# The head of a fused transformer kernel: products of zeros on PE, a held load, and norm weights behind the transposes

## The chip, the cores and the metric

The kernel runs on one core of a Trainium2 chip. The metric is the device time of one execution in microseconds (us), the median of several runs. The engines are PE (TensorE, matrix products), DVE (VectorE), ACT (ScalarE), POOL (GpSimd) and SP (SyncE, which here issues the loads). SBUF is the memory on the core with 128 partitions; PSUM is the memory that PE writes its results to.

## The reference

The input `x` has 256 tokens of width 1024. A first block computes a SwiGLU feed-forward, a mixer (a gated linear recurrence and a windowed attention side by side) and a second feed-forward, each with a norm ahead of it and one behind it; a second block of two hybrid layers follows. The change touches only the beginning, which is

```python
def rms_norm(x, g):
    xf = x.astype(jnp.float32)
    y = xf * lax.rsqrt(jnp.mean(xf * xf, axis=-1, keepdims=True) + NORM_EPS)
    return (y * g.astype(jnp.float32)).astype(x.dtype)

def swiglu(x, w_gu, w_down):
    g, u = jnp.split(x @ w_gu, 2, axis=-1)
    return (jax.nn.silu(g) * u) @ w_down
...
    f = swiglu(rms_norm(h, ffn1_pre_g[l]), ffn1_w_gu[l], ffn1_w_down[l])
    h = h + MACARON_SCALE * rms_norm(f, ffn1_post_g[l])
```

with `w_gu` of 1024 x 5632 and `w_down` of 2816 x 1024, all in float32.

## The kernel before

The work runs in five phases: feed-forward, mixer, feed-forward, and two hybrid layers. The 256 tokens are two token tiles, t = 0 and 1, of 128 tokens each, whose residual stays in SBUF as `h0` and `h1`. Each phase normalizes a tile (`pre_norm`), transposes it on PE (`to_xT`), and then streams the weights from HBM in units of 512 KB.

Every product of two matrices is made of three (`mm3`, lines 224 to 226). An operand a is split into a rounded part ah (type fp32r, which PE multiplies in one pass) and the rest al = a - ah; the sum ah bh + ah bl + al bh takes the place of a b. For the weights this split is in `split_raw`: ACT casts the raw unit to its high part (line 207), DVE subtracts to get the low part (line 208). For the activations it is in `split` (lines 214 and 215). In the trace `raw` is a loaded unit, `w` its two parts, `xh` and `xl` the two parts of the transposed activations, `tp` the transposes in PSUM. There are 4 raw buffers and 8 w buffers, so unit 4 is loaded when the first raw buffer is free again.

The order on each engine is made by a scheduler. It takes the instructions by their place in the program, but lets a later one go ahead on an engine as long as the earlier one isn't ready by the scheduler's own account of time. Each engine then runs its instructions strictly in that order, and so does SP with its loads. `tc.issue_after(ins)` puts what a block traces on the engine of `ins` behind `ins` in that order; it adds no wait.

At the head of the program, `setup` loads tile 0 of x in two halves of 512 columns and the norm weights `ffn1_pre_g` as a broadcast, the same 4 KB row to all 128 partitions (`g`, 512 KB), and makes the identity for the transposes. `pre_norm(0)` squares on ACT (line 401), takes an inverse root on DVE in eight small operations (`root`), and multiplies h by the root and g on DVE (line 380, `hn`). `to_xT(0)` makes eight transposes on PE (line 391), four to a PSUM bank, and splits each bank into xh and xl.

The first feed-forward begins in `firstA` with two chunks of 512 columns, `ga` (gate) and `ua` (up), each with four units of 256 rows of `w_gu`. A unit is six products of 512 columns for each token tile. With `LEAD = 2` the program multiplies units 0 and 1 with token tile 0 first, then transposes tile 1, multiplies units 0 and 1 with tile 1, and takes the later units with both tiles in turn. Behind the chunks come pairs of 256 columns (`gu`), whose results stay transposed, and the down products (`dn`). When a chunk of ga is complete for a tile, ACT applies Silu to it (line 509). `run` walks through the generator of a phase with `next(cur)`: the first call loads the first units, the second multiplies the lead for tile 0, the third the rest.

The functions that the diff touches, with their callers:

Of the kernel before, what the change touches and what calls it, by code (L numbers as in the profile page):

```python
# [10 lines left out]
F32 = mybir.dt.float32  # L11
F32R = mybir.dt.float32r
I32 = mybir.dt.int32
AF = mybir.ActivationFunctionType
ALU = mybir.AluOpType
PSUM = bass.MemoryType.PSUM
P = 128
S = 256
D = 1024
# [3 lines left out]
SC = (1024 / 27) ** 2  # L23
EPS = 1e-6
# [7 lines left out]
AHEAD = 6  # L32
M_ORDER = 'xaxAxlxpPqLQ'
W_Q, W_C, W_D0, W_D = (10., 12., 14., 10.)
L_ORDER = 'v0mmma1b'
LEAD = 2
B_AFTER = 3
W_LRU, W_ML = (6.0,6.0)

# [3 lines left out]
NX = 3  # L43
W_SD = 8.0
W_X = 2.5


def host_constants():
# [48 lines left out]
class Kern:  # L97
    def __init__(self, tc, a, ex):
# [11 lines left out]
        self.now, self.live, self.last = 0.0, 0, None  # L110
        self.taken = deque([-W_X] * NX)
        self.lanes = {n: deque() for n in ("tp", "T", "S")}
# [37 lines left out]
    def room(self, n=1):  # L150

        while self.taken[n - 1] + W_X > self.now:
            yield 0.0, 0.3
# [85 lines left out]
    def root(self, v):  # L239

        nc = self.nc
        m = v.shape[1]
        s, t, p = (self.small([P, m], x) for x in ("rs", "rt", "rp"))
        stt, tt = nc.vector.scalar_tensor_tensor, nc.vector.tensor_tensor
        nc.vector.tensor_scalar(s.bitcast(I32), v.bitcast(I32), -0.5, float(0x5F3759DF - 2 ** 31), op0=ALU.mult, op1=ALU.add)

        def vss():
            if m == 1:  # L250
                stt(t, in0=s, scalar=v, in1=s, op0=ALU.mult, op1=ALU.mult)
            else:
                tt(t, s, s, op=ALU.mult)
                tt(t, t, v, op=ALU.mult)

        vss()
        stt(p, in0=t, scalar=-10.0 / 3, in1=t, op0=ALU.add, op1=ALU.mult)
        stt(s, in0=p, scalar=5.0, in1=s, op0=ALU.add, op1=ALU.mult)
        vss()
        stt(s, in0=t, scalar=-64.0 / 3, in1=s, op0=ALU.add, op1=ALU.mult)  # L260
        return s


    def setup(self):
        nc, a = self.nc, self.a
        c = self.const
        self.h = [c.tile([P, D], F32, name=f"h{t}") for t in range(2)]
        self.load_x(0)
        self.g_first = self.bcast(a["ffn1_pre_g"][0], "g0")
        self.id = c.tile([P, P], F32, name="ident")  # L270
        make_identity(nc, self.id)
        self.slots = {}

    def load_x(self, t):
        for f in range(2):
            c = slice(f * 512, (f + 1) * 512)
            self.nc.sync.dma_start(out=self.h[t][:, c], in_=self.a["x"][0, t * P:(t + 1) * P, c])

    def params(self):
        nc, a = self.nc, self.a  # L280
# [83 lines left out]
        xl = self.xp.tile([P, 8, S], F32R, tag="xl", name="xl")  # L364
        return xh, xl

    def pre_norm(self, t, g, late=False):

        nc = self.nc
        h = self.h[t]  # L370
        hn = self.b4([P, D], "hn")
        parts = [slice(q * 512, (q + 1) * 512) for q in range(2)]
        v = self.mean_square([h[:, c] for c in parts])
        if not late:
            for c in parts:
                nc.vector.tensor_tensor(hn[:, c], h[:, c], g[:, c], op=ALU.mult)
        rs = self.root(v)
        for c in parts:
            if late:
                ins = nc.vector.scalar_tensor_tensor(hn[:, c], in0=h[:, c], scalar=rs, in1=g[:, c], op0=ALU.mult, op1=ALU.mult)  # L380
            else:
                ins = nc.vector.tensor_scalar(hn[:, c], hn[:, c], rs, None, op0=ALU.mult)
            self.normed = ins.ins
        return hn

    def to_xT(self, t, hn, xT):
        sl = slice(t * P, (t + 1) * P)
        for q in range(2):
            ps = self.bank("x", "tp", (P, 4, P))
            for i in range(4):  # L390
                self.nc.tensor.transpose(ps[:, i], hn[:, (4 * q + i) * P:(4 * q + i + 1) * P], self.id)
            ins = self.split(xT[0][:, 4 * q:4 * q + 4, sl], xT[1][:, 4 * q:4 * q + 4, sl], ps)
        return ins

    def mean_square(self, parts):

        nc = self.nc
        ss = self.small([P, 2], "ss2")
        for i, x in enumerate(parts):
            junk = self.t([P, 512], "junk")  # L400
            nc.scalar.activation(junk, x, AF.Square, accum_out=ss[:, i:i + 1])
        v0, v = self.small([P, 1], "v0"), self.small([P, 1], "v")
        nc.vector.tensor_scalar(v0, ss[:, 0:1], SC / D, SC * EPS, op0=ALU.mult, op1=ALU.add)
        nc.vector.scalar_tensor_tensor(v, in0=ss[:, 1:2], scalar=SC / D, in1=v0, op0=ALU.mult, op1=ALU.add)
        return v

# [31 lines left out]
    def firstA(self, xT, chunks, evacs, lead=None):  # L438

        us = [(i, u) for i in range(len(chunks)) for u in range(4)]
        n0 = len(us) if lead is None else lead
        ws, accs = {}, {}
        for at, (i, u) in enumerate(us[:n0 if lead is None else 1]):

            with self.tc.issue_after(self.normed) if at >= AHEAD else nullcontext():
                ws[i, u] = chunks[i][0](u)
        yield

        def step(i, u, t):
            if (i, u) not in ws:
                ws[i, u] = chunks[i][0](u)
            if u == 0:
                accs[i, t] = self.bank("acc", chunks[i][2], (P, chunks[i][1]))
            self.stepA(accs[i, t], xT, ws[i, u], u, t)
            if u == 3:
                evacs(i, t, accs[i, t])

        for i, u in us[:n0]:  # L460
            step(i, u, 0)
        yield
        for i, u in us[:n0]:
            step(i, u, 1)
        for i, u in us[n0:]:
            for t in range(2):
                step(i, u, t)
# [671 lines left out]

    def run(self, out, stop=99):  # L1140
        nc, a = self.nc, self.a
        self.setup()
        ffn = lambda n, **kw: (FFN_POOLS, lambda x: self.ffn(x, a[f"ffn{n}_w_gu"][0], a[f"ffn{n}_w_down"][0], **kw))
        layer = lambda l: (LAYER_POOLS, lambda x: self.layer(l, x))
        phases = [(ffn(1, lead=LEAD, early=self.params), "ffn1_post_g", 0.5, a["mix_pre_g"][0]), ((MIXER_POOLS, self.mixer), "mix_post_g", 1.0, a["ffn2_pre_g"][0]),
                  (ffn(2), "ffn2_post_g", 0.5, a["norm_g_2"][0]), (layer(0), None, 0, a["norm_g_2"][1]), (layer(1), None, 0, None)]
        xT = self.new_xT()
        hn = [self.pre_norm(0, self.g_first, True)]
        chain = lambda t, acc: self.pre_norm(t, self.g_first, True)
        acc = None  # L1150
        cur = None
        for i, ((pools, start), post, scale, pre) in enumerate(phases):

            ph = self.phase(pools)
            ph.__enter__()
            cur = start(xT)
            next(cur)
            ins = self.to_xT(0, hn[0], xT)
            if i == 0:
                self.load_x(1)  # L1160
            with self.tc.issue_after(ins) if i == 0 else nullcontext():
                hn.append(chain(1, acc))
            next(cur)
            self.to_xT(1, hn[1], xT)
            acc = next(cur)
            if i == stop - 1 or i == len(phases) - 1:
                if post is None:
                    self.residual(0, acc, out)
                    self.residual(1, next(cur), out)
                else:  # L1170
                    gp = self.bcast(a[post][0], "gpost")
                    self.post_norm(0, acc, gp, scale)
                    self.post_norm(1, next(cur), gp, scale)
                    for t in range(2):
                        nc.sync.dma_start(out=out[t * P:(t + 1) * P], in_=self.h[t])
                ph.__exit__(None, None, None)
                return
            gp = self.bcast(a[post][0], "gpost") if post else None
            gn = self.bcast(pre, "gpre")

            def chain(t, acc, gp=gp, gn=gn, scale=scale):
                if gp is None:
                    self.residual(t, acc)
                else:
                    self.post_norm(t, acc, gp, scale)
                return self.pre_norm(t, gn)

            xT = self.new_xT()
            hn = [chain(0, acc)]
            acc = next(cur)  # L1190
            ph.__exit__(None, None, None)
# [138 lines left out]
```

## Time and profile before

| what | us |
|---|---|
| median of 3 runs | 1348.41 |
| lowest, highest | 1348.16, 1349.8 |
| the profiled execution | 1345.55 |
| its span, from the first to the last instruction | 1343.8 |

The profiled execution is one execution of its own beside the three runs; its span leaves out 1.75 us of its time. In the views below an instruction is named by engine, line of the program, operation and operands (written first, read behind the arrow), a shape and a count; a bracket tells how long its engine idled ahead of it, and what ended that. PEld is the load of the stationary operand on PE, which overlaps the products. A q behind an engine is its queue.

### The profile page before, as it was taken

What the parts mean: (1) busy time and instruction counts of PE and PEld (TensorE: products, weight loads), DVE (VectorE), ACT (ScalarE), POOL (GpSimd) and SP (SyncE); (2) the same over time, 40 slices, a digit from 0 to 9 for tenths busy, and PEclk for the clock granted to TensorE, in tenths of its full rate; (3) what the DMA queues carried; (4) which work ended last, traced back from release to release, by engine and by line L of the source; (5) the groups of instructions that cost most, each with busy time, mean ns of one, the idle gap of its engine ahead of it and who ended that gap; (6) DMA issues with size and microseconds to landing.
All of it is one profiled execution on the core that took longest, in us unless ns stands there. A gap on an engine that the chain in (4) does not pass through costs nothing.

```text
span 1343.8 us, 24690 instructions
## 1 busy us (share of the span) xinstructions
PE 1313.7 (98%) x9434; PEld 1215.6 (90%) x9434; DVE 948.5 (71%) x2178; ACT 784.5 (58%) x1468; POOL 3.0 (0%) x10
## 2 busy tenths in 40 slices
PE   6999999999999999999999999999999999999998
PEld 5899988989997899998998889999899988899997
DVE  6547667897868655568888676666788886765663
ACT  6444544788745544455667776554456667755451
POOL 0000000000000000000000000000000000000000
PEclk9999999999999999999999999999999999999999
DMA  7757764445565566673755454666656543546661
GB/s 255 226 166 234 224 219 142 139 146 135 169 213 179 176 197 191 205 231 98 212 142 131 126 173 126 180 186 194 179 157 186 142 128 104 173 145 187 193 195 52
DMA packets 234806, 230.30 MB, mean 171 GB/s; under 512 B 12336, under 2 KB 213184, under 8 KB 234688
## 3 DMA queue, kind: packets, MB, share of 16 engines
q1 hardware_dynamic: 232432, 227.05, 56.8%
q10 hardware_dynamic: 2256, 1.67, 0.5%
q8 instruction: 74, 1.21, 0.4%
q14 instruction: 44, 0.36, 0.1%
HBM read 227.64 MB, written 1.05 MB: 170 GB/s over the span
## 4 chain that ended last, share of the span: by engine, by line
PE 75%; DVE 11%; ACT 6%; DMA 5%; issue 2%; SPq 0%; ACTq 0%; DVEq 0%
PE gu L224 5%; PE gu L226 5%; PE gu L225 5%; PE gp L224 3%; DVE w L208 3%; PE gp L225 3%; PE gp L226 3%; PE dqk L224 3%; PE dqk L226 3%; PE dn L226 3%; PE dn L225 3%; PE dqk L225 3%; PE dn L224 3%; DMA raw<-in_w_in_dram 3%; PE po L224 2%
## 5 line engine op out<-in xcount | busy, mean ns | idle before, releaser
L208 DVE TENSOR_TENSOR w<-raw,w 128x1024 fp32r<-128x1024 f32 (+1 forms) x437 | 501.8, 1156 | 222.3 <-ACT w L207 218.5
L207 ACT CAST w<-raw 128x1024 fp32r<-128x1024 f32 (+1 forms) x437 | 433.3, 999 | 334.4 <-PE gu L226 51.1
L224 PE MATMUL gu<-xh,w 128*128 128x256 f32 x576 | 159.6, 277 | 0.0
L226 PE MATMUL gu<-xh,w 128*128 128x256 f32 x576 | 159.2, 276 | 0.0
L225 PE MATMUL gu<-xl,w 128*128 128x256 f32 x576 | 159.1, 276 | 0.0
L224 PE MATMUL dqk<-w,xh 128*128 128x384 f32 x384 | 136.5, 355 | 0.0
L225 PE MATMUL dqk<-w,xh 128*128 128x384 f32 x384 | 129.5, 337 | 0.0
L226 PE MATMUL dqk<-w,xl 128*128 128x384 f32 x384 | 129.2, 336 | 0.0
L225 PEld LDWEIGHTS gu<-xl,w 128*128 128x128 f32 x576 | 108.2, 188 | 0.6
L224 PEld LDWEIGHTS gu<-xh,w 128*128 128x128 f32 x576 | 108.1, 188 | 0.6
L224 PE MATMUL gp<-xh,w 128*128 128x256 f32 x384 | 108.3, 282 | 0.0
L226 PEld LDWEIGHTS gu<-xh,w 128*128 128x128 f32 x576 | 108.2, 188 | 0.0
L226 PE MATMUL gp<-xh,w 128*128 128x256 f32 x384 | 106.4, 277 | 0.0
L225 PE MATMUL gp<-xl,w 128*128 128x256 f32 x384 | 106.2, 277 | 0.0
L224 PEld LDWEIGHTS dqk<-w,xh 128*128 128x128 f32 x384 | 72.2, 188 | 6.2 <-issue 6.0
L224 PEld LDWEIGHTS gp<-xh,w 128*128 128x128 f32 x384 | 72.1, 188 | 2.7 <-issue 2.7
L225 PEld LDWEIGHTS dqk<-w,xh 128*128 128x128 f32 x384 | 72.4, 189 | 0.2
L226 PEld LDWEIGHTS gp<-xh,w 128*128 128x128 f32 x384 | 72.2, 188 | 0.0
L226 PEld LDWEIGHTS dqk<-w,xl 128*128 128x128 f32 x384 | 72.2, 188 | 0.0
L225 PEld LDWEIGHTS gp<-xl,w 128*128 128x128 f32 x384 | 72.2, 188 | 0.0
L226 PE MATMUL dn<-w,aT 128*128 128x512 f32 x176 | 69.1, 393 | 0.0
L225 PE MATMUL dn<-w,aT 128*128 128x512 f32 x176 | 68.9, 391 | 0.0
(378 smaller groups left out, 3242.6 us busy)
## 6 DMA issues: line engine op xcount, KB each, us to landing
raw<-in_w_in_dram SPq DMA_DIRECT2D x140, 512.0 KB
raw<-in_ffn_w_gu_dram SPq DMA_DIRECT2D x88, 512.0 KB
raw<-in_w_in_dram SPq DMA_DIRECT2D x192, 192.0 KB
raw<-in_ffn_w_down_dram SPq DMA_DIRECT2D x44, 512.0 KB
raw<-in_w_o_dram SPq DMA_DIRECT2D x16, 512.0 KB
raw<-in_w_proj_attn_dram SPq DMA_DIRECT2D x16, 256.0 KB
raw<-in_w_proj_lru_dram SPq DMA_DIRECT2D x8, 512.0 KB
raw<-in_w_out_dram SPq DMA_DIRECT2D x8, 512.0 KB
```

Of the source, the lines that this page charges most:

```text
L207: nc.scalar.copy(hi, raw)
L208: nc.vector.tensor_tensor(lo, raw, hi, op=ALU.subtract)
L224: m(out, lhsT=ah, rhs=bh, start=first, stop=False)
L225: m(out, lhsT=ah, rhs=bl, start=False, stop=False)
L226: self.last = m(out, lhsT=al, rhs=bh, start=False, stop=last).ins
```

## The change

- In `setup` the norm weights come as an 8 x 128 tile. PE transposes it to 128 x 8, and ACT copies it to `gT`, in which each partition has the weights of its eight columns of the transposed activations.
- `pre_norm` in the first phase only multiplies by the root, on ACT. The weights are applied in `to_xT`: DVE multiplies each bank of four transposes by `gT` into an SBUF tile `xg`, from which xh and xl are made.
- A tile of zeros is made on DVE. `spin(n)` multiplies it n times with itself on PE (128 x 128 by 128 x 256, float32); nobody reads the results. `SPIN` gives the counts: 2 at the start, 4 behind the transpose of the norm weights, 1 behind the transposes of tile 0, and 2, 1, 2, 2 behind the four units of the lead.
- `LEAD` is 4: all of ga is multiplied with tile 0 ahead of the transposes of tile 1. Unit 0 is loaded at the first `next(cur)`, units 1 and 2 at the second, in SP's order behind the load of tile 1 of x.
- The load of tile 1 of x comes behind two memsets of one column each of `h1`, which DVE runs behind the first small operation of tile 0's root.

```diff
-LEAD = 2
+LEAD = 4
+SPIN = (2, 4, 1, 2, 1, 2, 2)
...
 in root():
-        stt(s, in0=t, scalar=-64.0 / 3, in1=s, op0=ALU.add, op1=ALU.mult)
+        self.rooted = stt(s, in0=t, scalar=-64.0 / 3, in1=s, op0=ALU.add, op1=ALU.mult).ins
...
 in setup():
-        self.g_first = self.bcast(a["ffn1_pre_g"][0], "g0")
+        g = self.t([8, P], "g8")
+        nc.sync.dma_start(out=g, in_=a["ffn1_pre_g"][0].rearrange("(k p) -> k p", p=P))
         self.id = c.tile([P, P], F32, name="ident")
         make_identity(nc, self.id)
+        self.zero = self.tl("n", [P, 256], "zero")
+        nc.vector.memset(self.zero, 0.0)
+        self.spin(SPIN[0])
+        gp = self.bank("x", "gT", (P, 8))
+        self.last = nc.tensor.transpose(gp, g, self.id[0:8, 0:8]).ins
+        self.spin(SPIN[1])
+        return gp
+
+    def spin(self, n):
+        ps = self.bank("yp", "spin", (P, 256))
+        for _ in range(n):
+            with self.tc.issue_after(self.last) if self.last is not None else nullcontext():
+                self.nc.tensor.matmul(ps, lhsT=self.zero[:, 0:P], rhs=self.zero, start=True, stop=True)
...
 in pre_norm():
-            if late:
-                ins = nc.vector.scalar_tensor_tensor(hn[:, c], in0=h[:, c], scalar=rs, in1=g[:, c], op0=ALU.mult, op1=ALU.mult)
+            if g is None:
+                nc.scalar.activation(hn[:, c], h[:, c], AF.Copy, scale=rs)
...
 in to_xT():
+            src = ps
+            if gT is not None:
+                self.last = tr.ins
+                src = self.t([P, 4, P], "xg")
+                self.nc.vector.tensor_tensor(src, ps, gT[:, ks].unsqueeze(2).to_broadcast([P, 4, P]), op=ALU.mult)
+            ins = self.split(xT[0][:, ks, sl], xT[1][:, ks, sl], src)
...
 in firstA():
-        for at, (i, u) in enumerate(us[:n0 if lead is None else 1]):
+        for at, (i, u) in enumerate(us[:n0 if lead is None else 3]):
-            with self.tc.issue_after(self.normed) if at >= AHEAD else nullcontext():
+            with self.tc.issue_after(self.normed) if at >= AHEAD or lead is not None and at == 0 else nullcontext():
                 ws[i, u] = chunks[i][0](u)
+            if lead is not None and at == 0:
+                yield
         yield
...
-        for i, u in us[:n0]:
+        for at, (i, u) in enumerate(us[:n0]):
             step(i, u, 0)
+            if lead is not None:
+                self.spin(SPIN[3 + at])
...
 in run():
-        self.setup()
+        gp = self.setup()
...
-        hn = [self.pre_norm(0, self.g_first, True)]
-        chain = lambda t, acc: self.pre_norm(t, self.g_first, True)
+        gT = self.const.tile([P, 8], F32, name="gT")
+        nc.scalar.copy(gT, gp)
+        hn = [self.pre_norm(0, None)]
+        self.normed = self.rooted
+        chain = lambda t, acc: self.pre_norm(t, None)
+        with self.tc.issue_after(self.squared):
+            for f in range(2):
+                nc.vector.memset(self.h[1][:, f * 512:f * 512 + 1], 0.0)
...
             next(cur)
-            ins = self.to_xT(0, hn[0], xT)
             if i == 0:
                 self.load_x(1)
+            ins = self.to_xT(0, hn[0], xT, gT)
+            if i == 0:
+                self.spin(SPIN[2])
+                with self.tc.issue_after(ins), self.tc.issue_after(self.loaded):
+                    next(cur)
             with self.tc.issue_after(ins) if i == 0 else nullcontext():
                 hn.append(chain(1, acc))
-            next(cur)
-            self.to_xT(1, hn[1], xT)
+            with self.tc.issue_after(ins) if i == 0 else nullcontext():
+                next(cur)
+            self.to_xT(1, hn[1], xT, gT)
+            gT = None
```

`self.squared` is the first small operation of `mean_square` on DVE, `self.loaded` the load of the second half of tile 1.

## Rows read from the trace of the kernel before

**Rows 1.** The page's busy line: busy us, share of the span, instructions.

```profile
PE 1313.7 (98%) x9434; PEld 1215.6 (90%) x9434; DVE 948.5 (71%) x2178; ACT 784.5 (58%) x1468; POOL 3.0 (0%) x10
```

**Rows 2.** Timeline, PE, 9 to 20 us: start, us, engine, line, what.

```profile
9.65 1.94 PE L391 MATMUL tp<-ident,hn 128*128 128x128 f32 x8 [9.65 <-DVE hn L380]
...
11.56 0.80 PE L224 MATMUL ga<-w,xh 128*128 128x512 f32 x1
...
13.53 0.63 PE L224 MATMUL ga<-w,xh 128*128 128x512 f32 x1
...
13.96 0.63 PE L225 MATMUL ga<-w,xh 128*128 128x512 f32 x1
...
16.09 0.50 PE L225 MATMUL ga<-w,xh 128*128 128x512 f32 x1 [0.65 <-DVE w L208]
...
16.43 0.40 PE L226 MATMUL ga<-w,xl 128*128 128x512 f32 x1
...
18.27 1.07 PE L391 MATMUL tp<-ident,hn 128*128 128x128 f32 x8
...
19.55 0.51 PE L224 MATMUL ga<-w,xh 128*128 128x512 f32 x1
```

**Rows 3.** The same timeline, SP's issues, ACT and DVE, 0 to 13 us.

```profile
0.74 0.86 SPq L277 DMA_DIRECT2D h<-in_x_dram  x2
...
1.65 0.42 SPq L182 DMA_DIRECT2D g<-in_ffn_pre_g_dram  x1
2.12 0.43 SPq L188 DMA_DIRECT2D raw<-in_ffn_w_gu_dram  x1
2.59 1.04 SPq L277 DMA_DIRECT2D h<-in_x_dram  x2
3.46 0.63 ACT L401 ACTIVATE junk<-h 128x512 f32<-128x512 f32 x1 [1.45 <-DMA h<-in_x_dram]
...
4.11 0.63 ACT L401 ACTIVATE junk<-h 128x512 f32<-128x512 f32 x1
...
4.87 0.16 DVE L404 SCALAR_TENSOR_TENSOR v<-ss,v 128x1 f32<-128x1 f32 x1 [0.49 <-ACT junk L401]
...
6.14 0.16 DVE L260 SCALAR_TENSOR_TENSOR rs<-rt,rs 128x1 f32<-128x1 f32 x1
8.76 1.41 DVE L380 SCALAR_TENSOR_TENSOR hn<-h,rs,g 128x512 f32<-128x512 f32 x2 [2.46 <-DMA g<-in_ffn_pre_g_dram]
...
9.98 1.05 ACT L207 CAST w<-raw 128x1024 fp32r<-128x1024 f32 x1 [5.15 <-DMA raw<-in_ffn_w_gu_dram]
10.93 1.29 ACT L214 CAST xh<-tp 128x512 fp32r<-128x512 f32 x2
11.06 1.23 DVE L208 TENSOR_TENSOR w<-raw,w 128x1024 fp32r<-128x1024 f32 x1 [0.89 <-ACT w L207]
...
12.20 1.28 DVE L215 TENSOR_TENSOR xl<-tp,xh 128x512 fp32r<-128x512 f32 x2
```

**Rows 4.** Busy time by stretch, instructions of ga alone (count, clock, DMA share).

```profile
11.50:18.30 6.80, 6.09 (x16) 3.63 (x16) 0.00 (x0) 1.00 0.66 209
```

**Rows 5.** Groups by line on PE, 11.5 to 37.8 us.

```profile
L224 PE MATMUL ga<-w,xh 128*128 128x512 f32 x16 | 7.3, 454 | 0.0
...
L226 PE MATMUL ua<-w,xl 128*128 128x512 f32 x16 | 6.3, 394 | 0.0
```

**Rows 6.** Timeline, PE, 37 to 38 us.

```profile
37.76 0.28 PE L224 MATMUL gu<-xh,w 128*128 128x256 f32 x1
```

**Rows 7.** Timeline, PE, around 258 us.

```profile
257.74 0.59 PE L838 MATMUL lg<-xc,wab 128*128 128x256 f32 x2
258.17 0.59 PE L839 MATMUL lg<-xc,wab 128*128 128x256 f32 x2
```

**Rows 8.** The first timeline again, ACT, 25 to 27 us.

```profile
25.52 1.28 ACT L509 ACT_TABLE_LOAD   x1
...
26.82 0.60 ACT L509 ACTIVATE sa<-ga 128x512 f32<-128x512 f32 x1
```

More of the change, by code (lines that the diff above doesn't have):

```diff
@@ L268, in setup @@
         self.load_x(0)
-        self.g_first = self.bcast(a["ffn1_pre_g"][0], "g0")
+        g = self.t([8, P], "g8")
+        nc.sync.dma_start(out=g, in_=a["ffn1_pre_g"][0].rearrange("(k p) -> k p", p=P))
         self.id = c.tile([P, P], F32, name="ident")
         make_identity(nc, self.id)
-        self.slots = {}
+        self.zero = self.tl("n", [P, 256], "zero")
[10 more added lines that the diff above has]
+                self.nc.tensor.matmul(ps, lhsT=self.zero[:, 0:P], rhs=self.zero, start=True, stop=True)
     def load_x(self, t):
@@ L276, in load_x @@
             c = slice(f * 512, (f + 1) * 512)
-            self.nc.sync.dma_start(out=self.h[t][:, c], in_=self.a["x"][0, t * P:(t + 1) * P, c])
+            self.loaded = self.nc.sync.dma_start(out=self.h[t][:, c], in_=self.a["x"][0, t * P:(t + 1) * P, c]).ins
     def params(self):
@@ L365, in new_xT, with pre_norm @@
         return xh, xl
-    def pre_norm(self, t, g, late=False):
+    def pre_norm(self, t, g):
         nc = self.nc
@@ L373, in pre_norm @@
         v = self.mean_square([h[:, c] for c in parts])
-        if not late:
+        if g is not None:
             for c in parts:
@@ L378, in pre_norm, with to_xT @@
         for c in parts:
-            if late:
-                ins = nc.vector.scalar_tensor_tensor(hn[:, c], in0=h[:, c], scalar=rs, in1=g[:, c], op0=ALU.mult, op1=ALU.mult)
-            else:
-                ins = nc.vector.tensor_scalar(hn[:, c], hn[:, c], rs, None, op0=ALU.mult)
-            self.normed = ins.ins
+            if g is None:
+                nc.scalar.activation(hn[:, c], h[:, c], AF.Copy, scale=rs)
+            else:
+                self.normed = nc.vector.tensor_scalar(hn[:, c], hn[:, c], rs, None, op0=ALU.mult).ins
         return hn
-    def to_xT(self, t, hn, xT):
+    def to_xT(self, t, hn, xT, gT=None):
         sl = slice(t * P, (t + 1) * P)
         for q in range(2):
+            ks = slice(4 * q, 4 * q + 4)
             ps = self.bank("x", "tp", (P, 4, P))
             for i in range(4):
-                self.nc.tensor.transpose(ps[:, i], hn[:, (4 * q + i) * P:(4 * q + i + 1) * P], self.id)
-            ins = self.split(xT[0][:, 4 * q:4 * q + 4, sl], xT[1][:, 4 * q:4 * q + 4, sl], ps)
+                tr = self.nc.tensor.transpose(ps[:, i], hn[:, (4 * q + i) * P:(4 * q + i + 1) * P], self.id)
+            src = ps
[4 more added lines that the diff above has]
+            ins = self.split(xT[0][:, ks, sl], xT[1][:, ks, sl], src)
         return ins
@@ L402, in mean_square @@
         v0, v = self.small([P, 1], "v0"), self.small([P, 1], "v")
-        nc.vector.tensor_scalar(v0, ss[:, 0:1], SC / D, SC * EPS, op0=ALU.mult, op1=ALU.add)
+        self.squared = nc.vector.tensor_scalar(v0, ss[:, 0:1], SC / D, SC * EPS, op0=ALU.mult, op1=ALU.add).ins
         nc.vector.scalar_tensor_tensor(v, in0=ss[:, 1:2], scalar=SC / D, in1=v0, op0=ALU.mult, op1=ALU.add)
```

## The prediction

> **What bounds the kernel now.** I read the page's busy shares first, then the timeline of the first 45 us engine by engine, then the count and the spacing of the first phase's products, and last single rows for prices. The page says that PE is busy for 1313.7 us of 1343.8 [rows 1]; 30 us are left, and the first 9.65 of them lie ahead of PE's first instruction [rows 2]. So a change to the head can give back some of these 9.65 us and what is lost until PE runs without gaps, and nothing else.
>
> The head is a chain [rows 3]. The x tile lands and the squares begin at 3.46; the root is done at 6.14 + 0.16 = 6.30; then DVE waits 2.46 us for the broadcast of g, which was issued at 1.65, and multiplies from 8.76; PE transposes from 9.65 [rows 2]. Unit 0 of the weights is cast only from 9.98, 7.9 us after its issue at 2.12, since x's second tile and g are under way beside it. The casts of xh come next, from 10.93, and the first product starts at 11.56 [rows 2].
>
> PE's clock: the clock column reads 1.00 even for 11.5 to 18.3 [rows 4], so here the starts must tell. Starts of products of 512 columns lie 0.43 us apart at 13.53 and 13.96, which is 1.2 GHz; the eight from 16.43 to the transposes at 18.27 lie 0.23 apart, which is 2.4. Just ahead of the change PE stood 0.65 us for DVE's w, until 16.09 [rows 2].
>
> Now an account that I can repeat for the changed kernel. The two chunks ga and ua are 2 x 3 lines x 16 = 96 products [rows 5]. Sixteen start by 18.3 [rows 4], the other 80 fill 19.5 to 37.76, where the gu products begin [rows 6]: 18.26 / 80 = 0.228 us each, with no gap. So 37.76 = 11.56 (first start) + 96 x 0.228 (21.9) + 8 transposes of the second tile (0.9 [rows 2]) + **3.4 us of loss**, 2.9 of them before 16.09 (seven products in 4.53 us, which would be 1.6 at 2.4 GHz). Behind 37.76 PE is the bound, with waits that do not know when the phase began; I take the time at which gu begins as the measure, and let its shift go through to the end.
>
> **The change, part by part.**
>
> *g goes behind the transposes.* Removed: a 512 KB broadcast and the 2.46 us wait for it. Added: an 8 x 128 load, one transpose, one copy. When the small load lands no row shows; the x halves take 2.7 us from issue to use (0.74 to 3.46), g's broadcast 7.1 (1.65 to 8.76) [rows 3]. It is nearest to the first in kind, so I take 4.2, behind x, whose second half is in use at 4.11. The multiplication moves from DVE (1.41 us for two) to ACT, 2 x 0.6 by the rows of Square and of xh [rows 3], and a DVE multiplication out of PSUM comes between transposes and cast: 0.64 for a half, by xl, which also reads PSUM [rows 3]. That part lengthens the chain by 0.65 us and costs DVE nothing in sum (1.41 off, about 1.3 on).
>
> *x's second tile waits.* Its two loads wait for two memsets on DVE, queued behind the first of the small root operations, some 4.4 us; DVE has a hole of 0.49 there, ahead of 4.87 [rows 3]. SP is in order, so units 1 to 3 stand behind it and leave at 5.5 to 6.5, some 2 us later than now, when x's second tile leaves at 2.59 [rows 3]. Unit 0 then has only x's first tile ahead of it. It lands between 5.4 (an estimate: right behind x's 4.11, with the 1.3 us or so that two halves of x need) and 9.96 (as now); I take 6. It is needed by 8.8, so this is hidden with 2.5 us to spare. Unit 1 I expect by 9.5; it is cast behind xh anyway.
>
> *Spins.* The tile of zeros is plain fp32. The nearest rows are the products lg, fp32 on both sides with 256 columns: each stands as two pieces, and the pair starts 0.43 us after the pair ahead, at 2.4 GHz [rows 7]; 0.85 at 1.2. So the six in the setup are 5.1 us of PE at most, and the eight behind them 0.43 each if the clock is up. Two run from about 1.1 to 2.8, the transpose of g at 4.2, four more until 7.9. None holds h's transposes long, as hn comes at 6.30 + 0.6, or + 1.05 more if ACT casts unit 0 first: 7.0 to 8.0.
>
> *First product.* Transposes from 7.9, half of them 0.45 to 0.9 (0.11 or up to 0.24 each, 1.07 or 1.94 for eight [rows 2]): 8.5. Multiplication 0.64: 9.2. Cast 0.6: 9.9 with the semaphores. Bounds: 9.3, with the clock up by 6 us; 11.0, if ACT casts unit 0 behind hn or the clock is late. I take **9.9, 1.7 us ahead of 11.56**.
>
> *LEAD 4.* 24 products of the first token tile now stand ahead of the second tile's transposes, in place of 12 by the program and 16 in the trace. They need units 0 to 3. DVE, from 9.2: one more multiplication, two xl of 0.64, then one w of 1.23 for each unit: w of unit 1 at about 12.8, unit 2 at 14.0, unit 3 at 16.5 with the second tile's root between. PE needs them at 12.3, 14.4 and 16.6: it waits for unit 1 alone, some 0.4, and for the first xl 0.4. ACT, from 9.2, has two casts of xh, three of 1.05, the squares (1.6) and hn (1.2), 7.2 us in all: done by about 18 with its waits.
>
> *Seven spins inside the lead* (2, 1, 2, 2) cost 7 x 0.43 = **3.0 us of PE**; the one ahead of the first product is hidden in the 1.4 us of multiplication and cast. This is the dear part: at 2.4 GHz there is hardly a wait for them to fill.
>
> *Silu moves.* With four units in the lead ga of the first tile is finished at about 18, and its Silu with the table load comes just ahead of the second tile's casts. The rows show 1.28 us for the load and the Silu right behind it at 26.82, so 1.9 us with it [rows 8]; the transposes run at 18.8, the multiplication ends at 20.0, so ACT is free in time. The Trainium skill (ScalarE: Activation LUTs, What ACT_TABLE_LOAD costs) puts a switch of table at about 2.66 us, with a drain beside the load of 1283 ns; the row agrees on the load and shows no drain. What a longer switch would do stands under rival B.
>
> *Second tile.* From its transposes to its first product 2.0 us, of which 0.9 is transposes. Products of unit 4 can fill the rest, if w is there; half filled, 0.5.
>
> **Sum.** 9.9 + 21.9 + 0.9 + 3.0 + waits (0.4 + 0.4 + 0.5, less the part of the spins that lies in a wait, 0.3: 1.0) = 36.7, against 37.76: **1.1 us earlier**. The profiled execution took 1345.55 with its span of 1343.8, so 1.75 around it; it becomes 1344.45, span 1342.7. The median of the three runs is 2.9 above that execution, and 1348.4 - 1.1 = **1347.3**.
>
> **The rivals.**
>
> *A. More comes back* (0.2). If the first product starts at 9.3 and every wait holds a spin, the sum is 35.1 + waits near 0: 2.7 us earlier; a changed order of DVE's and ACT's work from 37 us on could add some tenths. 1344.5 to 1345.8. For it: units 1 to 3 come some 3 us sooner and DVE has slack after 20 us. Against: the spins' 3.0 us are fixed.
>
> *B. No change at all* (0.2): the small load or the held tile takes back the 1.7 us. PE is in order: g's transpose, then four spins, then h's transposes. If g lands at 5.9 in place of 4.2, the first product is back at 11.6; the lead's spins then make it 0.6 later than before in sum. Likewise, if the memsets come behind DVE's first w, at 7.8, units 1 to 3 land some 3 us later and PE waits 2 us for unit 1. 1348 to 1349.6. Against: x's halves show no such delay, and DVE has its hole at 4.4. A third way, 0.03 of the 0.2: the switch to Silu holds ACT for two loads of 1.28 us; the second tile's casts and its first product then come 1.3 us later, the sum is 38.0, the time 1348.6. Against it stands the one row, with Silu right behind the load. (The Trainium skill's page named above would have it so.)
>
> *C. The clock does not stay up* (0.1, slower). PE waits for g from 2.8 to 4.2 and idles around 9; now it ran at 1.2 GHz from 9.65 to 16 with gaps of that size. If it does so through the lead, 24 products cost 0.2 more each and seven spins 0.43: 4.8 + 3.0, less 1.1 of covered waits: 6.7 later than my sum, 1354. It decides from half a unit on: six products and two spins cost 2.1, twice the gain. With two units cold it is 1350.5 to 1351.5.
>
> **Chances and range.** The forecast, 0.2 to 2.2 us earlier, has 0.5: 1346.2 to 1348.2. A measurement of this kernel cannot tell under about 0.2%, 2.7 us, from no change: 1345.7 and 1351.1 are the edges. Of A 0.17 and of the forecast's own tail 0.04 lie below 1345.7; of C 0.07 above 1351.1. So faster 0.21, same 0.72, slower 0.07. Leaving out 0.1 on either side, the range is 1344.4 to 1350.0.
>
> **What the changed profile would show.** hn on ACT from about 6.4 to 8, and no wait for g; unit 0 cast by 7; spins of 0.85 up to about 7.9 and of 0.43 inside the lead; starts of products 0.23 apart from the first one at 9.9; 24 ga products before the second transposes at 18.8; gu beginning at 36.7. I am wrong if the lead's spins stand inside waits of DVE's w (then w is later than I think and the spins are free), if the spacing is 0.43 past 11, if g's transpose comes after 5, or if the shift at gu is not the shift at the end.

## The result, and the profile after

The changed kernel takes 1363.6 us (median of 6 runs, 1357.8 to 1364.3), the one before 1348.5 beside it: a ratio of **1.010** with a 95% interval of 1.008 to 1.0121. It is slower by 15 us, where 1 us faster was forecast; the range ended at 1350.0.

The page of the changed kernel, its span and busy line, to be read beside [rows 1]:

```profile
span 1362.0 us, 24754 instructions
PE 1334.2 (98%) x9463; PEld 1234.4 (91%) x9463; DVE 949.9 (70%) x2181; ACT 787.7 (58%) x1473; POOL 3.0 (0%) x10
```

The span grew by 18.2 us, and PE was busy for 20.5 us more. It has 29 records more than before, the 14 products of zeros (two records each) and the transpose of g, together 9.7 us (2.1 and 3.8 in the setup, 0.6 ahead of the first product, 3.0 in the lead, 0.2 for g); the other 11 us are work that was there before, taking longer. So this is no story of waits alone.

The head, from the timeline of the changed kernel (columns as in [rows 2, 3]):

```profile
4.33 0.24 PE L280 MATMUL gT<-ident,g 8*128 8x8 f32 x1 [1.07 <-DMA g<-in_ffn_pre_g_dram]
4.38 0.07 DVE L1182 MEMSET h<- 128x1 f32 x2
5.34 4.34 SPq L190 DMA_DIRECT2D raw<-in_ffn_w_gu_dram  x4
...
6.99 1.04 ACT L209 CAST w<-raw 128x1024 fp32r<-128x1024 f32 x1 [2.12 <-DMA raw<-in_ffn_w_gu_dram]
7.94 1.33 ACT L397 ACTIVATE hn<-h,rs 128x512 f32<-128x512 f32 x2
8.71 1.85 PE L408 MATMUL tp<-ident,hn 128*128 128x128 f32 x8 [0.42 <-ACT hn L397]
9.93 1.35 DVE L413 TENSOR_TENSOR xg<-tp,gT 128x512 f32<-128x512 f32 x2 [0.64 <-PE tp L408]
10.66 1.28 ACT L216 CAST xh<-xg 128x512 fp32r<-128x512 f32 x2 [1.34 <-DVE xg L413]
11.33 0.50 PE L226 MATMUL ga<-w,xh 128*128 128x512 f32 x1 [0.34 <-ACT xh L216]
...
18.95 1.33 ACT L397 ACTIVATE hn<-h,rs 128x512 f32<-128x512 f32 x2
19.52 1.02 PE L289 MATMUL spin<-zero 128*128 128x256 f32 x4
20.31 1.28 ACT L535 ACT_TABLE_LOAD   x1
20.38 1.04 PE L408 MATMUL tp<-ident,hn 128*128 128x128 f32 x8
21.60 0.60 ACT L535 ACTIVATE sa<-ga 128x512 f32<-128x512 f32 x1
22.09 1.98 ACT L209 CAST w<-raw 128x1024 fp32r<-128x1024 f32 x2
23.97 1.14 ACT L216 CAST xh<-xg 128x512 fp32r<-128x512 f32 x2
24.64 0.80 PE L226 MATMUL ga<-w,xh 128*128 128x512 f32 x1 [3.23 <-ACT xh L216]
```

The wait for g is gone, as meant. But hn stands on ACT behind the cast of unit 0, and the first product comes 0.23 us earlier than before, not 1.7. Then the second tile: its xh stands on ACT behind Silu and **two weight casts** (22.09 to 24.07), and PE idles 3.23 us. Behind that idle time the clock falls. The windows of PE in the head (us, busy and instructions, granted clock):

```profile
core 0: us, PE busy (x), PEclk, DMA share, GB/s
11.50:20.00 8.50, 8.50 (x37) 1.00 0.79 255
20.00:25.00 5.00, 1.77 (x12) 0.90 0.82 278
25.00:31.00 6.00, 6.00 (x15) 0.52 0.58 178
31.00:44.00 13.00, 13.00 (x58) 1.00 0.74 235
```

Up to 20 the clock held (inside a unit the products start 0.23 us apart, from 12.39 on); from 25 to 31 PE ran at 1.2 GHz, 15 products instead of 26. So gu begins at 44.08, 6.3 us later than before.

And the head is not all. The same instruction in both traces, start in us:

| first of | before | after | later by |
|---|---|---|---|
| ga | 11.56 | 11.33 | -0.23 |
| gu | 37.76 | 44.08 | 6.32 |
| pf (conv weights) | 98.15 | 104.50 | 6.35 |
| tp of the mixer | 199.18 | 207.91 | 8.73 |
| gu, second feed-forward | 454.01 | 464.06 | 10.04 |
| bz | 656.91 | 669.12 | 12.21 |
| po, first hybrid layer's second stage | 900.10 | 912.71 | 12.61 |
| o of that layer | 954.50 | 969.25 | 14.75 |
| po, second layer's second stage | 1263.58 | 1279.51 | 15.93 |
| o of that layer | 1317.98 | 1336.05 | 18.07 |

Twelve microseconds come behind the start of gu, where the order of instructions is the same in both kernels (PE, ACT, POOL and SP throughout; DVE from 1 us behind that start on). Two kinds of step are seen. Some lie at waits at which the clock fell again: of the changed kernel,

```profile
384.00:390.00 6.00, 4.41 (x24) 0.72 0.57 176
657.00:663.00 6.00, 5.41 (x22) 0.72 0.61 184
```

The others have neither a wait nor a lower clock. The same stretches of PE, as windows, first of the kernel before, then of the changed one; the middle row lies between two groups of transposes, the last one is po of the second layer:

```profile
1237.00:1241.70 4.70, 4.70 (x43) 1.00 0.50 169
1242.00:1252.00 10.00, 10.00 (x90) 1.00 0.66 178
1264.00:1314.00 50.00, 50.00 (x443) 1.00 0.65 190
```

```profile
1252.30:1257.00 4.70, 4.70 (x42) 1.00 0.39 135
1257.30:1267.30 10.00, 10.00 (x87) 1.00 0.69 178
1280.00:1330.00 50.00, 50.00 (x427) 1.00 0.64 187
```

PE has no gap and its full clock in all six, yet it starts 443 products in 50 us before and 427 after: one each 113 ns, or one each 117. I took this from start to start over the whole trace (products of 256 columns; a stretch counts as slow where most of 13 neighbours are over 116 ns): the pace goes over from one to the other at transposes and waits and then holds, up to 84 us without a break. Before, 165 us run at the slower pace; after, 368. The 203 us more, at 16 products in 443, are **7.3 us**.

What differs behind the head is where things lie. gT, 8 columns of float32, is allocated behind the identity, so all SBUF tiles that follow (constants, raw, w, activations) stand 32 bytes further than before.

### The profile page after: what moved, and what is told of

The parts are those of the page before. It is cut to its first block, busy times and chain, and to the rows that moved or that the text cites. A ratio compares the mean times of both kernels' runs of the same rounds, so it can differ in the third digit from the quotient of the medians.

```text
span 1362.0 us, 24754 instructions
## 1 busy us (share of the span) xinstructions
PE 1334.2 (98%) x9463; PEld 1234.4 (91%) x9463; DVE 949.9 (70%) x2181; ACT 787.7 (58%) x1473; POOL 3.0 (0%) x10
## 4 chain that ended last, share of the span: by engine, by line
PE 79%; DVE 8%; ACT 5%; DMA 5%; issue 2%; ACTq 0%; SPq 0%; DVEq 0%
PE gu L226 5%; PE gu L228 5%; PE gu L227 5%; PE dqk L226 4%; PE dqk L228 4%; PE dqk L227 4%; PE gp L226 3%; PE gp L227 3%; PE gp L228 3%; DVE w L210 3%; PE dn L228 3%; PE dn L227 3%; PE dn L226 3%; PE po L226 2%; DMA raw<-in_w_in_dram 2%
```

## Experiments

**The 32 bytes, both ways.** First the changed kernel with gT put into a tile `gap` that the kernel has and never uses, so that all other tiles stand as before:

```diff
-        pool("gap", 1).tile([P, 32], F32, name="gap")
+        self.gap = pool("gap", 1).tile([P, 32], F32, name="gap")
...
-        gT = self.const.tile([P, 8], F32, name="gT")
+        gT = self.gap[:, 0:8]
```

> The changed kernel, but gT lies in the unused tile named gap, so that every other tile of SBUF stands at its address of before; in the changed kernel all of them behind the identity stand 32 bytes further on. The order of the instructions on all engines is that of the changed kernel. Theory 1 (addresses): the 11.7 us that the changed kernel loses behind the start of gu come from the 32 bytes; gu starts at 44 as in the changed kernel, the end comes 6 to 8 us later than before, 1354.5 to 1356.5, and products of 256 columns lie 0.113 us apart from 105 to 185 and in the ends of both layers, where the changed kernel has 0.118. Rival (timing: the later start of gu meets the clock and the other engines differently): 1357 to 1364 as the changed kernel, with stretches of 0.118 as long as there.

Measured: 1350.26 us, ratio 1.0017 (1.0002 to 1.0032). Then the kernel before with an unused tile and nothing else:

```diff
         make_identity(nc, self.id)
+        self.pad = c.tile([P, 8], F32, name="pad")
```

> The kernel before with one unused tile of 32 bytes behind the identity and nothing else: the order on all engines is that of before. Theory 1 (addresses): the head is that of before, and the stretches of 0.118 us between products of 256 columns grow as in the changed kernel: 7 to 11 us slower than before, 1355 to 1360. Rival (timing): 1348.5, within 2 us.

Measured: 1357.57 us, ratio 1.0061 (1.0037 to 1.0085), 296 us at the slower pace. So most of the loss has nothing to do with what the change does: 32 unused bytes cost 8 us, and the change without them is within 0.3% of before.

In that first run PE stalls at the second tile as in the changed kernel (3.4 us), but its clock did not fall behind the stall, and gu begins at 41.49. Nor did it fall in a second trace of the changed kernel itself (the last run under *The identity*; stall 3.5 us, gu at 41.93). The window behind the stall, with gT in `gap` and in that second trace:

```profile
25.00:31.00 6.00, 6.00 (x27) 1.00 0.69 193
```

```profile
25.00:31.00 6.00, 5.68 (x25) 1.00 0.61 187
```

In the two runs with the identity moved (also below, stalls of 3.4 us) it fell again, and gu begins at 43.62 and 43.38. The order is the same in all five, so such a fall comes in one execution and not in another: three of five here. With the stall alone gu is some 4 us later than in the trace of before, with the fall about 6.

**ACT's order.** Silu of the first tile and the casts of units from the fifth on come behind the second tile's xh (`hold` leaves Silu out of the lead and runs it after the transposes):

```diff
-            if u == 3:
+            if u == 3 and not hold:
                 evacs(i, t, accs[i, t])
...
-            self.to_xT(1, hn[1], xT, gT)
+            ins = self.to_xT(1, hn[1], xT, gT)
             gT = None
-            acc = next(cur)
+            with self.tc.issue_after(ins) if i == 0 else nullcontext():
+                acc = next(cur)
```

> The changed kernel with the Silu of the first token tile and the casts of units 4 and later put behind the second tile's casts of xh on ACT. Theory 2 (the head): PE stands 3.2 us at 21.4 because ACT has the table load, the Silu and two casts of w ahead of xh, and then runs at 1.2 GHz from 24.0 to 30.8; with ACT in the other order the wait is 1 us or less, the clock stays up, and gu starts at 37 to 38.5: 5.5 to 7 us faster than the changed kernel, 1356.5 to 1358. Rival (the spins and the long lead are the cost): gu starts at 42 or later, a gain of 2 us or less, 1361.5 or more.

> Both edits: gT in the unused tile, and ACT's order. If theories 1 and 2 hold, the two gains add: 1346 to 1349, gu at 37 to 38.5 and stretches of 0.118 us as before. If only the head's holds, 1356.5 to 1358; if only the addresses', 1354.5 to 1356.5.

Measured: 1360.93 (ratio 1.009, 1.0073 to 1.0107) with the displaced tiles, 1351.75 (1.0026, 1.0016 to 1.0037) without. Neither is faster, clear of noise, than its partner without this order (1.010 and 1.0017). The stall of 3.2 us falls to 1.0 and gu begins at 39.67 and 38.69. But then, in the waits of PE in the first 60 us of the second of these,

```profile
engine line waited for: us in total, times, longest us
PE aTp L521 <- DVE aT L217: 2.6, 1, 2.6
PE ga L226 <- ACT xh L216: 1.6, 2, 1.0
```

the casts put off are missing at the next transposes (`aTp`, 0.6 us in the kernel before), and 2.0 us go there; from the start of gu to pf this run takes 64.08 us, the one with gT in `gap` alone 60.27. The stall is real and the order makes it, but repairing it this way only moves it.

**How large a displacement.** As the 32 bytes above, with tiles of 16 and 32 columns, 64 and 128 bytes.

> The kernel before with an unused tile of 64 bytes a partition in place of the 32 of the shift alone: every later SBUF tile stands 64 bytes further, so again on multiples of 64; the order on all engines is that of before. Theory 1 (it is the rest of the address by 64 that counts): 1348.4 +- 2, the stretches of 256-column products at 118 ns in place of 113 stay at some 170 us in all. Rival (any displacement costs, whatever its size): 1355 to 1359 with some 300 us of such stretches, as with 32 bytes.

> The kernel before with 128 unused bytes behind the identity. If the cost depends on the rest of the displacement by 128 (of 64 it does not, as the run with 64 bytes showed): 1348 to 1351. If any displacement of the tiles against the identity costs: 1356 to 1360, with 300 to 430 us at the slower pace.

Measured: 1358.84 (1.0063, 1.0047 to 1.0079) and 1357.37 (1.0054, 1.0036 to 1.0071), each with some 315 us at the slower pace. My first theory, multiples of 64, fell: any of the three displacements behind the identity costs 7 to 9 us.

**Which distance.** With more or less in `gap`, which lies behind the weights, the weights and the activations move against each other: first `gap` alone, then pad and `gap` together, pad by 8, 16 and 32 columns.

```diff
-        pool("gap", 1).tile([P, 32], F32, name="gap")
+        pool("gap", 1).tile([P, 40], F32, name="gap")
...
+        self.pad = c.tile([P, 8], F32, name="pad")
...
-        pool("gap", 1).tile([P, 32], F32, name="gap")
+        pool("gap", 1).tile([P, 24], F32, name="gap")
```

> The kernel before, the unused tile gap 32 bytes longer: raw and w stay where they were, all tiles behind them (hn, aT, xh, xl, cn, sa, sq, w2 and the rest) stand 32 bytes further. Theory 1a (the activations that PE reads, and what ACT and DVE write beside them, carry the cost): 1355 to 1358, all of the 9.3 us. Theory 1b (the weights w and raw carry it): 1347 to 1350. If each carries a part: 1351 to 1354 here and in the run that shifts the weights alone.

> The kernel before with 32 unused bytes ahead of raw and w and 32 bytes less in gap behind them: the constants behind ident, raw and w stand 32 bytes further, all later tiles where they were. Theory 1b (the weights carry the cost): 1355 to 1358. Theory 1a (the activations carry it): 1347 to 1350. A part each: 1351 to 1354.

> The kernel before with 64 unused bytes ahead of raw and w and 64 less in gap: the weights move by 64 bytes against the activations and the identity, which keep their places. If only the rest by 64 of the distance between weights and activations counts: 1347 to 1353, no stretch at 118 ns or more over most of the kernel. If the rest by 128 counts as the 32 bytes did: 1368 to 1373. A time under 1345 would say that this distance is better than that of before.

> The kernel before with 128 unused bytes ahead of raw and w and no gap: the weights move by 128 bytes against the rest. If the distance counts by its rest by 64 or by 128: 1347 to 1353. If any change of it costs: 1356 to 1373.

Measured: 1372.37 (1.0158, 1.0141 to 1.0175) with the activations 32 bytes further; with the weights further by 32, 64 and 128 bytes 1369.96 (1.0144, 1.0121 to 1.0166), 1373.33 (1.0191, 1.0173 to 1.0209) and 1367.59 (1.0148, 1.013 to 1.0166). The first two were to tell whether weights or activations carry the cost; both cost twice what was expected for all of it, so it is neither alone but the distance between them. (In the first the activations also move against the identity.) By the other two it goes by no rest by 64 or 128, and no displacement tried was free. Here the slower pace is almost everywhere. The page of the kernel with the weights 64 bytes further, whose instructions and order are those of before:

```profile
PE 1346.1 (98%) x9434; PEld 1246.0 (91%) x9434; DVE 949.5 (69%) x2178; ACT 785.6 (57%) x1468; POOL 3.0 (0%) x10
```

PE is busy for 32 us more than in [rows 1], with the same 9434 records.

Then everything together, the unused tile ahead of the residual and the identity:

```diff
+        self.pad = c.tile([P, 8], F32, name="pad")
         self.h = [c.tile([P, D], F32, name=f"h{t}") for t in range(2)]
```

> The kernel before with the 32 unused bytes ahead of the residual and the identity, so that every tile the program allocates moves by 32 bytes together. Theory 2 (what counts is how the tiles stand to one another; the identity is PE's other operand in every transpose, and behind transposes the pace is set): 1348 to 1351 as before, stretches at the slower pace some 170 us and at the same places. Rival (the absolute address counts): 1355 to 1359, as when the identity stays.

Measured: 1352.13, ratio 1.0014 (1.0001 to 1.0027), the slow stretches from 820 us on those of before (443 products in 50 us of the last po). So, by this one displacement, absolute addresses matter little, distances do.

**The identity.** In the changed kernel, gT ahead of the residual and the identity; then gT between the two (the edit shown; in the first the new line stands ahead of `self.h`); then the changed kernel again beside that.

```diff
+        self.gTt = c.tile([P, 8], F32, name="gT")
         self.id = c.tile([P, P], F32, name="ident")
...
-        gT = self.const.tile([P, 8], F32, name="gT")
+        gT = self.gTt
```

> The changed kernel with gT allocated ahead of the residual in place of behind the identity: the weights, the activations and all other tiles stand where they stand in the changed kernel (32 bytes further than before), only gT, the residual and the identity differ; the order is that of the changed kernel. Theory 2 (the place of the identity against the tiles that are transposed decides which pace follows a transpose): 1350 to 1354, the pattern of slow stretches from 820 us on as in the kernel before. Rival (the absolute addresses of weights and activations decide): 1361 to 1364 as the changed kernel.

> The changed kernel with gT between the residual and the identity: against the changed kernel only gT and the identity move, the residual keeps its place. If the identity's place does it: 1350 to 1355, as with gT ahead of both, with 443 products in 50 us of the last po stage. If the residual's place does it: 1361 to 1364, with 427.

> The changed kernel itself, beside the run with gT between residual and identity on the same chip: 1361 to 1364, 427 products in 50 us of the last po stage, as before.

Measured: 1353.58 (1.0047, 1.003 to 1.0065); 1355.39 (1.0041, 1.0021 to 1.0061); 1361.17 (1.0088, 1.0066 to 1.011). Weights, activations and order are those of the changed kernel in all three. The page and the windows of the first, to be read beside those of the changed kernel above:

```profile
PE 1324.3 (98%) x9463; PEld 1224.4 (90%) x9463; DVE 949.6 (70%) x2181; ACT 788.5 (58%) x1473; POOL 3.0 (0%) x10
1246.20:1250.90 4.70, 4.70 (x43) 1.00 0.45 156
1251.20:1261.20 10.00, 10.00 (x90) 1.00 0.69 180
1273.20:1323.20 50.00, 50.00 (x443) 1.00 0.64 190
```

and the last po of the second and of the third:

```profile
1276.50:1326.50 50.00, 50.00 (x443) 1.00 0.62 190
```

```profile
1277.40:1327.40 50.00, 50.00 (x427) 1.00 0.61 187
```

Moving the identity by 32 bytes gives back 5.8 us on the same chip (1361.2 to 1355.4). PE's busy time falls by 10 us against the first trace of the changed kernel, but by 3.7 between the traces of these two runs (1329.9 to 1326.2), as it also holds the falls of the clock, four in the one and two in the other.

One stage of the hybrid layers shows the distances without that scatter: from a layer's first po to its first o, start to start. In any one trace both layers agree to 0.01 us:

| kernels | us in each layer |
|---|---|
| before; all tiles 32 bytes further; the changed kernel with gT in `gap`, or with the identity moved along (all nine traces) | 144.39 |
| changed, also with ACT's order; unused bytes behind the identity, 32, 64 or 128 (six traces) | 147.33 to 147.37 |
| weights and activations moved against each other (four traces) | 148.53 to 149.62 |

So the identity's distance alone takes 3.0 us in each of two layers, **6.0 us**, in every execution. Elsewhere the pace also differs between two executions of one kernel: from pf to the transposes of the mixer the changed kernel took 103.41 us in its first trace and 101.02 in its second (before 101.03). Which accesses meet, PE's own operands or those of other engines beside them, no run separates.

**The products of zeros.** Addresses as before, first without any of the 14, then without the seven in the lead (2, 4, 1, 0, 0, 0, 0), then this with ACT's order of above.

```diff
-SPIN = (2, 4, 1, 2, 1, 2, 2)
+SPIN = (0, 0, 0, 0, 0, 0, 0)
...
     def spin(self, n):
+        if n == 0:
+            return
```

> The changed kernel with gT in the unused tile gap (addresses as before) and none of its 14 products of zeros; without them the scheduler fills the lead with some ua products of tile 1 differently, but 24 products still stand ahead of the second transposes. Theory (the products hold PE's clock up and are worth what they cost): the first 10 to 16 products lie 0.43 us apart, 2 to 3 us lost at the start, 3.0 us of lead products saved: gu begins at 40 to 42, 1349.5 to 1351, no better than with them (1350.26). Rival (they only cost): products 0.23 apart from the first on or soon after, gu begins some 3 us earlier than at 41.49, time 1347 to 1348.

> The changed kernel with gT in gap (addresses as before) and without the seven products of zeros behind the lead's units; those of the setup stay. Theory (they cost 0.43 us each in full, and the stall for the second token tile keeps its length): gu begins 3.0 us earlier than 41.49, at 38.5; 1347.5 to 1349. Rival (they stand in waits that then come back as idle time, since the second tile's casts on ACT come no earlier): gu at 40 to 41.5 as without any spins (40.04), 1350 to 1351.5.

> The same, and Silu of the first tile and the casts of the units from 4 on behind the second tile's xh on ACT. Theory: the stall falls to 1 us, gu begins at 35.7 to 36.5, some 1.5 us before that of before, and 1 us of it is left at the end: 1346.5 to 1348. Rival (the later casts take it back at the transposes of aT, as in the runs with the order alone changed): gu early, but the next phase's first products 2 us or more later than before; 1349 to 1351.

Measured: 1351.54 (1.0014, 1.0001 to 1.0028), 1353.12 (1.002, 1.0002 to 1.0039) and 1351.43 (1.0008, 0.9995 to 1.0021); gu begins at 40.04, 40.47 and 39.26. Without any, the first products (the windows count those that began ahead of them) come so:

```profile
11.00:14.00 3.00, 2.78 (x7) 1.00 1.00 378
14.00:17.00 3.00, 3.00 (x9) 1.00 0.67 206
```

They start 0.43 us apart up to 16.95, 1.2 GHz by the starts. The lead's 24 products end at 19.9 (from 11.22 on); with the seven spins among them the lead takes 9.3 us (11.21 to 20.48, the run with gT in `gap`). Without the lead's spins alone the clock falls inside the lead,

```profile
14.00:18.00 4.00, 3.24 (x9) 0.58 0.67 207
```

and of the 3.0 us that they cost only 1.0 is left at gu (40.47 against 41.49). But these two runs change the order too. Without spins the scheduler puts Silu ahead of the second tile's hn on ACT, where it stood behind; in the run without any:

```profile
18.81 1.28 ACT L537 ACT_TABLE_LOAD   x1
20.10 0.60 ACT L537 ACTIVATE sa<-ga 128x512 f32<-128x512 f32 x1
20.59 1.32 ACT L399 ACTIVATE hn<-h,rs 128x512 f32<-128x512 f32 x2
```

PE then waits 1.5 us (1.3 in the second run) for hn ahead of the transposes and 0.8 in place of 3.4 for xh behind them. So gu's time there compares spins and order at once.

The third run and the one with gT in `gap` and ACT's order have the same order and differ in the seven spins alone. The lead takes 9.15 us with them (10.64 to 19.79) and 9.68 without (10.38 to 20.06), where PE waits 0.9 and 0.8 us for unit 1 and the clock falls:

```profile
15.00:18.40 3.40, 3.40 (x9) 0.50 0.72 211
```

gu begins at 38.69 with them and 39.26 without, and the times, 1.0026 and 1.0008, are not told apart. In all seven traces with the lead's spins the clock held through the lead; in both that have only the spins of the setup and the one ahead of the first product it fell. So the spins hold the clock, and what they hold is worth about what they cost. The third run's gu at 39.26 misses the 35.7 to 36.5 of its theory for the same reason. None of the kernels beats the one before.

## Why the prediction was wrong, point by point

*Right.* g's transpose at 4.33 (forecast 4.2), the memsets at 4.38 (4.4), the loads behind them at 5.34 (5.5 to 6.5), 24 products ahead of the second transposes, and the lead: 11.33 to 20.38 is 9.05 us, of which 24 x 0.228 = 5.5, spins 3.0, and 0.6 waits (0.4 and 0.4 by the forecast, less what spins fill). That length came out partly by luck: the spins are no fixed 3.0 on top, as the pair above has 9.15 with them and 9.68 without. The switch to Silu was one load of 1.28 us with Silu right behind it (20.31, 21.60), so rival B's third way did not happen. (The Trainium skill, ScalarE: Activation LUTs, What ACT_TABLE_LOAD costs, adds a drain to the load; this trace shows none.)

*The first product at 9.9* was 11.33. The bound of 11.0 named the cause, ACT's order of hn and the cast of unit 0, though the other way round (the paragraph on spins has that order too): the cast stood first in ACT's order, ACT stood idle for unit 0 until 6.99 though the root was done before that, and hn, ready to run by then, began at 7.94 (the forecast had up to 7.35). The transposes began at 8.71 in place of 7.9, and DVE's multiplication waited for them until 9.93, where the forecast had 8.5. Mis-sized by 1.4 us.

*"ACT is free in time"*, and 0.5 us for the second tile: this step failed. Silu did end at 22.2, half a microsecond behind the first half of the multiplication (21.02 + 0.64). But I asked only when ACT ends Silu, not what its order puts next, and that was two weight casts. The wait was 3.2 us, and the clock fell behind it. From the second transposes to the first product it took 4.3 us in place of 1.4, and the products behind it, 0.43 us apart up to 30.8, another 3.0: with the 1.4 of the first product these make gu 44.08 in place of 36.7. Rival C had the clock falling through the lead; it held there, and fell behind a stall that no rival had. In the second trace of the same kernel it did not fall, and gu began at 41.93.

*"Let its shift go through to the end"*: this is the step that failed most. gu came 6.3 us later, the end 18.1. The text gave a reason, that behind 37.76 "PE is the bound, with waits that do not know when the phase began". It took for granted that a product has one price, 0.228 or half of it. It has two, and in the trace after the dearer one holds for 203 us more. A tile allocated in the head chose it for 6.0 us of two stages in every execution; the rest of the 12 us behind gu differs from trace to trace. gT had a line in the change's list and no term in the sum. Nor are the waits behind gu the same (for cT, ahead of uq, PE waited 1.5 us before and 3.1 after).

*The account of before* rested on an early case. Of the nine traces with the order of before, which differ only in where tiles lie, gu begins at 37.76 and 37.55 in two and at 39.09 to 40.08 in seven, where the products stay 0.43 us apart until 19 us instead of 16. The trace of before, and that with 32 unused bytes:

```profile
16.50:18.20 1.70, 1.70 (x9) 1.00 0.49 80
```

```profile
16.50:18.20 1.70, 1.70 (x5) 1.00 0.86 199
```

The 3.4 us of loss, and the 6.3 by which gu came later, hang on which execution is taken for before.

In sum, by ratios: the change 1.0088 and 1.010 in its two measurements, the same with the identity moved along 1.0041 and 1.0047, with all tiles but gT in their old places 1.0017, with unused bytes alone 1.0054 to 1.0063. So of 11 to 15 us, 6 to 11 are the place of gT, 6.0 of them in the two stages above, and the rest, 2 to 6 us, the head and the falls of the clock that go with it. How that divides further stays open: the runs' intervals overlap, and falls of the clock behind later waits come in one execution and not in the next. Why a distance between operands sets PE's pace, and why 32, 64 and 128 bytes all cost, was not settled; only that it does.

## What to carry to other kernels

Ask of each new tile where it is allocated and what moves behind it: in a kernel that PE bounds, as here, 32 bytes can cost more than the edit saves; run the edit's allocation alone, with no new instruction, to see it. Where an edit lets work run sooner, read the whole order of the engine that the next step needs, not only the instruction that was moved. And a product that only holds the clock must cost less than the slow products that it spares: here 3.0 us against about as much.

## What the runs showed of the hardware

- Products of 256 columns at the full clock have two paces, 113 and 117 to 118 ns from start to start (443 or 427 in 50 us), and keep the one that they fall into behind transposes or a wait until the next ones.
- Which one depends on the distances in SBUF, and in some stages also on the execution: with the identity moved by 32 to 128 bytes against the tiles behind it, a stage of 144.39 us took 147.33 to 147.37, in each of six traces; the identity moved back gave back 6 us of 1361; weights moved by 32 to 128 bytes against the activations cost 19 to 26 us; all tiles moved together, under 3.
- Behind a PE stall of 3.2 to 3.5 us, with one order of instructions, the clock fell to 1.2 GHz in three executions and held in two; two of these, one of each kind, are of the same kernel.
